# Input units in pairs: seven block products for eight on the first four row tiles, weights in operands of two tiles

## The chip, the cores and the metric

One core of a Trainium2 chip runs the whole program. The metric is the device time of one execution in microseconds (us). Before the change it is 3091.2 us, the median of three runs (3088.71 to 3091.31). The profiled execution, from which every duration below is read, spans 3091.2 us as well.

## The reference, cut to what matters

Two layers of an encoder work on 768 tokens: a sample of 512 and a prompt of 256. All arithmetic is in fp32.

```
for l in range(2):
    h = rmsnorm(x, norm_pre[l])
    parts = split(h @ w_in[l])            # 2048 -> 56 units of 128 columns, and decays
    y_a = gated_delta_net(...)            # 4 heads, both directions, chunks of 64 tokens;
                                          # triangular_solve(I + a_low, ...) per chunk
    y_b = differential_attention(...)     # 4 heads, rotary, two softmaxes each
    y_c = b * dwconv3(c * x) * silu(z)    # 4 units of 128 channels
    y_m = attention(q, mem_k, mem_v)      # 4 heads; keys and values = rmsnorm(mem) @ w_kv
    x = x + rmsnorm(concat(y_a, y_b, y_c, y_m) @ w_out[l], norm_post[l])
```

The products h @ w_in, mem @ w_kv and y @ w_out have 2048 rows each, which is 16 row tiles of 128.

## The kernel before

**Products.** Activations lie with features on the partitions and tokens along the row. A *unit* is 128 output columns: 56 input units per layer (a list `UNITS` sets their order), 8 units for keys and values of the memory, 16 output units. Each fp32 operand is cut into a leading part `hi` and a remainder `lo` of TensorE's fp32r type, and a product of two is three products: hi·hi, hi·lo, lo·hi. For each of the 16 row tiles (`k`) of a unit TensorE (PE) so issues three products, and each of them twice, because a PSUM bank takes 512 columns: once over the sample's 512 tokens and once over the prompt's 256 (L220, `GROUPS`). One row tile of an input unit is three pairs of 512 and 256 columns. A unit's sums stay in PSUM (`pp`), from where the branches read them.

**Weights.** They come in quarters of four row tiles (128x512, 256 KB): SyncE (SP) issues the load (`raw`, L159), ScalarE (ACT) casts the leading part (`hi`, L170), and VectorE (DVE) subtracts it (`lo`, L181). `run_jobs` issues these a few quarters ahead of the products.

**Order.** Everything else is a set of Python generators. `tick()` lets each of them issue its next stage, and `run_jobs` calls it once per quarter of an input unit. So the work of the branches stands on each engine's queue at a place that is counted in quarters of products; each engine takes its queue in order, and where a row's input is late, the engine stands still and all behind it with it. `until()` ticks on without products where a product's input has not been issued yet.

**The inverse on GpSimd (POOL).** A head of the delta net needs inverses of unit triangles. PE's products at L738 close the matrices, DVE and POOL copy their 32x32 diagonal blocks (L783, L784), these go through DRAM (`ud`, `ul`) into a layout of 48 partitions, and POOL runs 30 rounds of a multiply (L796) and an add (L798) there, three rounds per tick. The result goes back through DRAM (`xd`, `c`), is copied into place (L820, L821, L822 to L825), and PE carries on with small products at L833. In the same stretch POOL does the rotary embedding of the next head of differential attention (L962, L965, L967) and the remainder of its keys (`bkl`, L1037), which PE reads at L1068.

**Memory attention.** `mem` loads a head's keys and values from DRAM (`mkv`), splits them (L1127, L1128), and makes three passes of 256 tokens: scores (L1151), maximum (L1154, L1155), exponentials (L1158), scaling (L1164), transposition (L1170) with split (L1172, L1173), product with the values (L1181), gate (L1183).

**Storage.** Parts of activations (`h`) have a pool of their own (`hp`), other tiles one of 25 slots (`wk`).

Of the kernel before, what the change touches and what calls it, by code (L numbers as in the profile page):

```python
# [52 lines left out]
NRAW = 4  # L53
NF = 3
TICK = 0.6


class Job:
    """Four quarters of products of one weight unit with the activations."""

    def __init__(self, src, segs, out, done=None, ready=None, start=None,
                 dense=False):
        self.src, self.segs, self.out, self.done, self.ready = src, segs, out, done, ready
        self.start, self.dense = start, dense
        self.w = [None] * 4


class Pair:
    """The accumulators of the two groups, where they are in separate tiles."""

    def __init__(self, new):
        self.new, self.t = new, {}

    def __getitem__(self, key):
        o = key[1].start
        if o not in self.t:
            self.t[o] = self.new()
        return self.t[o][:, 0:key[1].stop - o]
# [7 lines left out]
class Trunk:  # L86
    def __init__(self, ctx, tc, io):
# [3 lines left out]
        self.hp = ctx.enter_context(tc.tile_pool(name="hp", bufs=KT))  # L91
# [6 lines left out]
        self.jobs = []  # L98
        self.room = 4

# [10 lines left out]
    def ppt(self):  # L111
        return self.pp.tile([P, 1024], F32, tag="pp", name=self.nm("pp"))
# [7 lines left out]
    def hslot(self, g):  # L120
        return self.hp.tile([P, 2, GROUPS[g][1]], F32R, tag=f"h{g}", name=self.nm(f"h{g}"))

# [8 lines left out]
    def tick(self):  # L131
        """Issues the next stage of every background task that is due."""
# [21 lines left out]

    def wload(self, i):
        if i < len(self.quarters):
            job, q = self.quarters[i]
            rf = self.wp.tile([P, 4, P], F32, tag="raw", name=self.nm("raw"), bufs=NRAW)
            self.nc.sync.dma_start(rf, job.src[:, 4 * q:4 * q + 4, :])  # L159
            job.w[q] = rf  # L160

    def whi(self, i):
        """The leading part, in F32R, of a quarter of a weight unit."""
        if i >= len(self.quarters):
            return
        nc = self.nc
        job, q = self.quarters[i]
        rf = job.w[q]
        hi = self.wp.tile([P, 4, P], F32R, tag="hi", name=self.nm("hi"))
        nc.scalar.copy(hi, rf)  # L170
        job.w[q] = (rf, hi)

    def wlo(self, i):
        """What the leading part leaves of a quarter of a weight unit."""
        if i >= len(self.quarters):
            return
        nc = self.nc
        job, q = self.quarters[i]
        rf, hi = job.w[q]
        lo = self.wp.tile([P, 4, P], F32R, tag="lo", name=self.nm("lo"), bufs=3)  # L180
        nc.vector.tensor_tensor(lo, rf, hi.bitcast(F32), ALU.subtract)  # L181
        job.w[q] = (hi, lo)

    def run_jobs(self):
        nc = self.nc
        self.quarters = [(job, q) for q in range(4) for job in self.jobs[:2]]
        self.quarters += [(job, q) for job in self.jobs[2:] for q in range(4)]
        self.wload(0)
        self.tick()
        self.whi(0)  # L190
        self.wlo(0)
        nhi, nlo, nld = 1, 1, 4
        work = 1.0
        for i, (job, q) in enumerate(self.quarters):
            if q == 0 and job.start is not None:
                job.start()
# [1351 lines left out]
```

## Time and profile before

| | |
|---|---|
| median of three runs | 3091.2 us |
| span of the profiled execution | 3091.2 us |
| PE busy | 3004.3 us, 97% |
| DVE, ACT, POOL busy | 1591.0, 919.5, 879.3 us |
| chain that ended last, by engine | PE 81%, POOL 9%, DVE 4% |
| DMA | 269.83 MB, mean 87 GB/s |

A busy PE is not PE at its peak, because products are pipelined and their ends are modelled; the spacing of their starts tells what they cost. The chain of waits follows the work back from the last instruction: at each step to what released it, or else to the instruction before it on the same engine.

### The profile page before, as it was taken

What the parts mean: (1) busy time and instruction counts of PE and PEld (TensorE: products, weight loads), DVE (VectorE), ACT (ScalarE), POOL (GpSimd) and SP (SyncE); (2) the same over time, 40 slices, a digit from 0 to 9 for tenths busy, and PEclk for the clock granted to TensorE, in tenths of its full rate; (3) what the DMA queues carried; (4) which work ended last, traced back from release to release, by engine and by line L of the source; (5) the groups of instructions that cost most, each with busy time, mean ns of one, the idle gap of its engine ahead of it and who ended that gap; (6) DMA issues with size and microseconds to landing.
All of it is one profiled execution on the core that took longest, in us unless ns stands there. A gap on an engine that the chain in (4) does not pass through costs nothing.

```text
span 3091.2 us, 47316 instructions
## 1 busy us (share of the span) xinstructions
PE 3004.3 (97%) x18606; PEld 2604.7 (84%) x18606; DVE 1591.0 (51%) x2964; ACT 919.5 (30%) x1802; POOL 879.3 (28%) x1071
## 2 busy tenths in 40 slices
PE   8899999999999999999989999999999999999997
PEld 6778888888888888898867788888888888888886
DVE  6745455446345645632597554654563456455226
ACT  6422232222222232421234222322222222324112
POOL 4316214301601250310253260252117014303014
PEclk9899999999999999999999999999999999999998
DMA  6322222212212221532373222221222122224226
GB/s 236 115 69 64 62 60 81 54 56 76 75 53 72 75 57 49 169 99 65 119 246 108 65 60 62 65 79 50 74 75 64 54 69 76 57 74 152 62 62 232
DMA packets 170767, 269.83 MB, mean 87 GB/s; under 512 B 41584, under 2 KB 54128, under 8 KB 170544
## 3 DMA queue, kind: packets, MB, share of 16 engines
q1 hardware_dynamic: 169232, 265.48, 28.4%
q8 instruction: 146, 2.39, 0.3%
q10 hardware_dynamic: 1232, 1.07, 0.1%
q14 instruction: 77, 0.63, 0.1%
q0 software_dynamic: 80, 0.26, 0.0%
HBM read 233.97 MB, written 32.77 MB: 86 GB/s over the span
## 4 chain that ended last, share of the span: by engine, by line
PE 81%; POOL 9%; DVE 4%; issue 3%; DMA 1%; ACT 1%; SPq 0%; DVEq 0%; POOLq 0%; ACTq 0%
PE pp L220 69%; POOL ul L798 3%; POOL tl L796 3%; PE s L1091 1%; PE s L220 1%; DVE lo L181 1%; PE s L908 1%; PE s L528 1%; POOL bkl L1037 1%; PE s L934 1%; PE s L738 1%; PE s L921 1%; POOL sw L965 1%; PE s L1068 1%; PE s L1082 1%
## 5 line engine op out<-in xcount | busy, mean ns | idle before, releaser
L220 PE MATMUL pp<-h,hi 128*128 128x512 f32 (+1 forms) x9600 | 2185.7, 345 | 7.8 <-ACT h L364 6.3
L220 PEld LDWEIGHTS pp<-h,hi 128*128 128x128 f32 x9600 | 1513.2, 190 | 229.7 <-issue 8.8
L220 PE MATMUL pp<-h,lo 128*128 128x512 f32 (+1 forms) x4800 | 1316.0, 344 | 40.8 <-DVE lo L181 40.6
L220 PEld LDWEIGHTS pp<-h,lo 128*128 128x128 f32 x4800 | 766.2, 190 | 161.1 <-DVE lo L181 50.1
L181 DVE TENSOR_TENSOR lo<-raw,hi 128x512 fp32r<-128x512 f32 x700 | 567.5, 815 | 641.5 <-PE pp L220 430.0
L170 ACT CAST hi<-raw 128x512 fp32r<-128x512 f32 x700 | 429.7, 619 | 678.4 <-PE pp L220 562.3
L1354 POOL TENSOR_TENSOR acc<-acc,osq 128x768 f32<-128x768 f32 (+2 forms) x36 | 54.5, 1515 | 411.4 <-ACT osq L1347 403.7
L796 POOL TENSOR_TENSOR tl<-ul 48x30 f32<-48x30 f32 (+14 forms) x240 | 144.3, 601 | 90.2 <-DMA ul<-ud 59.6
L609 POOL TENSOR_TENSOR ao<-ao,hny 128x768 f32<-128x768 f32 x8 | 13.3, 1662 | 488.2 <-DVE so L605 430.9
L798 POOL TENSOR_TENSOR ul<-ul,tl 48x30 f32<-48x30 f32 (+14 forms) x240 | 146.1, 609 | 18.8
L1072 ACT ACTIVATE E<-s,bmx 128x512 f32<-128x512 f32 (+1 forms) x96 | 58.6, 614 | 201.6 <-DVE bmx L1071 190.9
L647 DVE SCALAR_TENSOR_TENSOR cva<-cv,gconv_s,cva 128x770 f32<-128x770 f32 x96 | 106.4, 1108 | 5.0
L1071 DVE TENSOR_REDUCE bmx<-s 128x1 f32<-128x512 f32 (+1 forms) x96 | 53.7, 596 | 80.5 <-PE s L1068 79.7
L679 POOL TENSOR_TENSOR gm<-masks_s,gr 128x768 fp32r<-128x768 f32 x32 | 53.9, 1712 | 118.3 <-DVE gr L565 118.3
L1339 DVE TENSOR_SCALAR ys<-pp,npost_s 128x768 f32<-128x768 f32 (+2 forms) x41 | 34.5, 841 | 98.1 <-PE pp L220 98.1
L923 ACT ACTIVATE x<-s,nD 128x128 f32<-128x128 f32 x96 | 33.6, 367 | 137.9 <-PE s L921 114.1
L725 POOL TENSOR_TENSOR U<-A,nD 128x768 f32<-128x768 f32 x16 | 27.4, 1734 | 152.1 <-DVE nD L721 152.1
L693 POOL TENSOR_SCALAR_AFFINE_SELECT A<-A 128x768 f32<-128x768 f32 x16 | 17.8, 1115 | 185.4 <-ACT A L691 185.4
L1347 ACT ACTIVATE osq<-pp 128x768 f32<-128x768 f32 (+2 forms) x38 | 25.8, 678 | 143.8 <-DVE ys L1339 143.6
L609 POOL TENSOR_TENSOR bo<-bo,hny 128x768 f32<-128x768 f32 x8 | 13.7, 1718 | 182.0 <-DVE hny L297 121.1
L1158 ACT ACTIVATE mE<-s,mmx 128x256 f32<-128x256 f32 x48 | 22.4, 471 | 131.3 <-DVE mmx L1155 129.3
L586 ACT ACTIVATE gate<-pp 128x768 f32<-128x768 f32 x32 | 26.0, 812 | 101.2 <-PE pp L220 101.2
(305 smaller groups left out, 2716.9 us busy)
## 6 DMA issues: line engine op xcount, KB each, us to landing
raw<-wu SPq DMA_DIRECT2D x472, 256.0 KB, 2.9
raw<-wo SPq DMA_DIRECT2D x164, 256.0 KB, 2.9
raw<-wkv SPq DMA_DIRECT2D x64, 256.0 KB, 4.1
y<-gate SPq DMA_DIRECT2D x24, 384.0 KB, 2.5
mem<-memT SPq DMA_DIRECT2D x32, 256.0 KB, 4.7
x<-xT SPq DMA_DIRECT2D x16, 384.0 KB, 5.3
yl<-y SPq DMA_DIRECT2D x24, 256.0 KB, 4.5
xl<-xT SPq DMA_DIRECT2D x16, 384.0 KB, 4.7
```

Source lines behind the costliest of these rows:

```text
L170: nc.scalar.copy(hi, rf)
L181: nc.vector.tensor_tensor(lo, rf, hi.bitcast(F32), ALU.subtract)
L220: nc.tensor.matmul(job.ps[:, o:o + n], w[:, j, :], job.H[g][k][:, x, :], start=(k == 0 and w is hi and x == 0), stop=(k == KT - 1 and w is ...
L647: nc.vector.scalar_tensor_tensor(a, cb[:, i:i + 770], w[:, i:i + 1], a, ALU.mult, ALU.add)
L679: nc.gpsimd.tensor_tensor(gms[d][x].rearrange("p (n c) -> p n c", n=NCH), masks[d].unsqueeze(1).to_broadcast([P, NCH, P]), dec["gs"][:, x, ...
L796: nc.gpsimd.tensor_tensor(t, ul[:, j + 1:, j:j + 1].to_broadcast([48, m, j]), ul[:, j:j + 1, 0:j].to_broadcast([48, m, j]), ALU.mult)
L798: nc.gpsimd.tensor_tensor(ul[:, j + 1:, 0:j], ul[:, j + 1:, 0:j], t, ALU.add)
L923: nc.scalar.activation(xt[:, ci, :], pb[:, ci * P:(ci + 1) * P], AF.Copy, scale=nD[:, d, n:n + 1])
L1071: nc.vector.tensor_reduce(mx[:, j:j + 1], pts[j][:, :ln], AX.X, ALU.max, negate=True)
L1072: nc.scalar.activation(E[j], pts[j][:, :ln], AF.Exp, bias=mx[:, j:j + 1], accum_out=sm[:, j:j + 1])
L1339: nc.vector.tensor_scalar(st["ys"][m][:, a:b], ps[:, a:b], self.npost[:, l, m:m + 1], None, ALU.mult)
L1354: nc.gpsimd.tensor_tensor(acc[:, o:o + n], acc[:, o:o + n], sq[:, o:o + n], ALU.add)
```

## The change

- **Halves.** The tokens are cut into two halves of 384 in place of 512 and 256. A plain row tile of an input unit is now three pairs of 384 and 384 columns.
- **Operands of two tiles.** Weights are loaded, cast and subtracted in pieces of two row tiles (128x256, 128 KB): loads L167, casts L189, subtractions L195. The list of work is now one of steps (`run_steps`), one operand each, and a tick comes when 0.6 of four row tiles' work has passed.
- **Seven products.** From the fifth unit on, input units are taken in pairs (26 per layer). The two units and the two halves of the tokens make a 2x2 block product with blocks of two row tiles for the first four row tiles. `pair_job` forms it in seven block products. It needs four sums of weight blocks (`wsum`, L182, on POOL), four combinations of activation blocks (`combine`, once per layer), and combinations of the results: copies on ACT (L308, L312), additions on DVE (L316, L321, L328, L331, L332) and two subtractions per pair on POOL (L317, L322). The other twelve row tiles are plain.
- **Copies out of PSUM.** Units no longer stay in PSUM for the branches: the combined unit lies in a slot (`u`), and the first four units are copied by ACT.
- **Storage.** One pool of 61 slots holds `h` and everything else. To make room, the delta net stores its matrices, keys, queries and values to DRAM and fetches them again (40 stores, 40 loads), transposes its keys twice, and memory attention waits (`turn`) while the last head of differential attention or the scans of a delta head are under way, and loads its keys and values only then.

The three places in the order of work that matter most follow. The first is POOL's queue at the end of the second delta head's inverse; before (`tl`, `ul` are the loop, `bkl` the remainder of keys, `U` and `w` the result):

```order
L796 TENSOR_TENSOR tl_4773<-ul_4771 48x30
L798 TENSOR_TENSOR ul_4771<-ul_4771,tl_4773 48x30
L801 AFFINE_SELECT ul_4771<-ul_4771 48x1024
L803 MEMSET ul_4771 48x32
L1037 TENSOR_TENSOR bkl_5206<-bk_4994,bks_5204 64x768
L1037 TENSOR_TENSOR bkl_5206<-bk_4994,bks_5205 64x768
L817 MEMSET w_912_5361 32x6x32
L818 MEMSET w_912_5361 32x6x32
L821 COPY U_4357<-c_900_5312 32x6x32 x4
```

and after, where L963 and L965 are the loop, L988 the copies, L1134 a rotary row that stood earlier:

```order
L963 TENSOR_TENSOR tl_5745<-ul_5743 48x30
L965 TENSOR_TENSOR ul_5743<-ul_5743,tl_5745 48x30
L1134 TENSOR_TENSOR u_6020<-u_6020,sw_6120 128x768
L968 AFFINE_SELECT ul_5743<-ul_5743 48x1024
L970 MEMSET ul_5743 48x32
L322 TENSOR_TENSOR uw_6044<-uw_6044 128x384
L182 TENSOR_TENSOR sum_6305<-raw_6235,raw_6237 128x256
L182 TENSOR_TENSOR sum_6307<-raw_6239,raw_6235 128x256
L182 TENSOR_TENSOR sum_6309<-sum_6305,raw_6239 128x256
L182 TENSOR_TENSOR sum_6311<-raw_6241,sum_6309 128x256
L1220 TENSOR_TENSOR bkl_6284<-u_6020,bks_6282 64x768
L1220 TENSOR_TENSOR bkl_6284<-u_6020,bks_6283 64x768
```

Five new rows, a combination of results and four weight sums, stand between the loop and the rows that PE reads; four more sums and two more combinations stand inside the loop.

The second is PE's queue where the first output unit of layer 0 meets the last passes of memory attention. In before the last product with the values (L1181) of the fourth head stands among the products of an input unit:

```order
L220 MATMUL pp_11664<-h_225_1035,lo_11660 128x256
L1181 MATMUL s_11785<-mPT_11703,mkvh_11496 128x256
L1181 MATMUL s_11785<-mPT_11704,mkvh_11496 128x256
L1181 MATMUL s_11785<-mPT_11703,mkv_11401 128x256
L1181 MATMUL s_11785<-mPT_11703,mkvh_11496 128x256
L1181 MATMUL s_11785<-mPT_11704,mkvh_11496 128x256
L1181 MATMUL s_11785<-mPT_11703,mkv_11401 128x256
L220 MATMUL pp_11664<-h_287_1256,hi_11658 128x512
```

and after, where L1335 are scores, L1354 transpositions and L1365 products with the values (one row of six is shown of some):

```order
L236 MATMUL pp_14417<-h_14408,lo_14438 128x384
L1354 MATMUL s_14513<-masks_s,mE_14461 128x128 x4
L1365 MATMUL s_14522<-mPT_14518,mkvh_14124 128x256
...
L1335 MATMUL s_14536<-mkvh_14532,mq_12984 128x256
...
L1354 MATMUL s_14554<-masks_s,mE_14547 128x128 x4
L1365 MATMUL s_14563<-mPT_14559,mkvh_14532 128x256
...
L236 MATMUL pp_14417<-h_14571,hi_14436 128x384 x2
```

The whole third pass, with its load of keys and values, now stands between the products of one output unit, with no other product of PE beside it.

The third is PE's queue in a pair. In before a row tile alternates the two groups of tokens:

```order
L220 MATMUL pp_11664<-h_287_1256,hi_11658 128x512
L220 MATMUL pp_11664<-h_226_1039,hi_11658 128x256
L220 MATMUL pp_11664<-h_287_1256,hi_11658 128x512
L220 MATMUL pp_11664<-h_226_1039,hi_11658 128x256
L220 MATMUL pp_11664<-h_287_1256,lo_11709 128x512
L220 MATMUL pp_11664<-h_226_1039,lo_11709 128x256
```

and after, the end of a plain row tile of the first unit, the seventh block product of the pair, and the start of a plain row tile of the second unit:

```order
L236 MATMUL pp_7536<-h_1507,lo_7657 128x384
L236 MATMUL pp_7536<-h_1348,lo_7657 128x384
L236 MATMUL pp_7509<-h_1598,hi_7655 128x384 x2
L236 MATMUL pp_7509<-h_1598,lo_7675 128x384
L236 MATMUL pp_7509<-h_1711,hi_7655 128x384 x2
L236 MATMUL pp_7509<-h_1711,lo_7675 128x384
L236 MATMUL pp_7509<-h_1403,hi_7673 128x384
L236 MATMUL pp_7509<-h_1098,hi_7673 128x384
```

A block product goes over one half of 384 columns alone (an `x2` counts two like rows), a plain row tile over both.

The core of the diff:

```diff
-NSLOT = 25
...
+TH = T // 2
+
+KS = 2
+NSLOT = 61
+NF = 2
 TICK = 0.6
...
+WBUFS = dict(raw=8, sum=4, lo=6)
+NHI = 6
+AHEAD = 5
...
+    def wsum(self, i):
+        st = self.steps[i]
+        for op in st.sums:
+            op.t = self.wtile(op, "sum")
+            self.nc.gpsimd.tensor_tensor(op.t, op.add[0].t, op.add[1].t, ALU.add)
+        self.held["raw"] -= len(st.sums) // 2
...
+        for i, st in enumerate(self.steps):
+            if st.start is not None:
+                st.start()
+            if work >= (0.3 if st.dense else TICK) or st.first:
                 self.tick()
                 work = 0.0
...
+            work += st.cost
+            upto("load", i + 1, self.wload)
...
+            upto("sum", min(i + AHEAD, 2 * i + 2), self.wsum)
+            upto("hi", min(i + AHEAD, 2 * i + 2), self.whi)
+            upto("lo", min(i + AHEAD - 1, 2 * i + 1), self.wlo)
+            upto("load", min(i + 2 * AHEAD, 2 * i + 5), self.wload)
+            if st.ready is not None:
+                self.until(st.ready)
+            op = st.op
+            terms = [(acc(), x, opens, closes) for acc, x, opens, closes in st.terms]
+            for j in range(op.n):
+                for w, part in ((op.hi, 0), (op.hi, 1), (op.lo, 0)):
+                    for acc, x, opens, closes in terms:
+                        nc.tensor.matmul(acc, w[:, j, :], x(j)[part],
...
+    def pair_job(self, srcs, H, B, done, start=(None, None), ready=None):
...
+        s1 = Operand(KS, add=(a21, a22))
+        s3 = Operand(KS, add=(a11, a21))
+        s2 = Operand(KS, add=(s1, a11))
+        s4 = Operand(KS, add=(a12, s2))
...
+        def after_p1():
+            nc.scalar.copy(u1()[:, 0:TH], ts[1][:, 0, 0:TH])
...
+        def after_p6():
+            u, w = u1()[:, TH:T], ts["w"]
+            nc.vector.tensor_tensor(w[:, TH:T], ts[1][:, 0, 0:TH], u1()[:, 0:TH], ALU.add)
+            nc.gpsimd.tensor_tensor(u, w[:, TH:T], w[:, 0:TH], ALU.subtract)
+
+        def after_p7():
+            w = ts["w"]
+            nc.vector.tensor_tensor(w[:, TH:T], ts[1][:, 0, 0:TH], w[:, TH:T], ALU.add)
+            nc.gpsimd.tensor_tensor(w[:, 0:TH], w[:, 0:TH], w[:, TH:T], ALU.subtract)
...
+        def product(op, get, x, opens, closes, after=None, **kw):
+            return Step(op, [(get, x, opens, closes)], op.n * 0.5 / 4, after=after, **kw)
...
+        steps = [product(a11, acc(1, 0), b11, True, True, after_p1, loads=[a21, a22, a11, a12], sums=[s1, s3, s2, s4],
+                         start=start[0], ready=ready, first=True),
+                 product(s1, acc(1, 1), bt("1"), True, True, after_p5, loads=[]),
+                 product(a12, acc(0, 0), b21, True, False, loads=[]),
+                 product(s2, acc(1, 0), bt("2"), True, True, after_p6, loads=[]),
+                 product(s4, acc(0, 1), b22, True, False, loads=[])]
+        steps += rest[0][:-1]
+        steps.append(product(s3, acc(1, 0), bt("3"), True, True, after_p7, loads=[]))
+        steps += rest[0][-1:]
+        steps.append(product(again, acc(1, 0), bt("4"), True, False, start=start[1], first=True))
+        steps += rest[1]
...
+    def combine(self, x1, x2, B):
...
+        nc.vector.tensor_tensor(t1, b12, b11, ALU.subtract)
+        nc.gpsimd.tensor_tensor(t3, b22, b12, ALU.subtract)
+        nc.vector.tensor_tensor(t2, t1, b22, ALU.subtract)
+        nc.vector.tensor_tensor(t4, b21, t2, ALU.add)
...
+    def turn(self):
+
+        while self.busy:
+            yield 0
...
-        while "q" not in st or "kv" not in st:
+        while "q" not in st:
             yield 0
-        q, kv = st["q"], self.mem_kv_split(st["kv"])
+        yield from self.turn()
+        kv = self.mem_kv(l, h, 0)
+        yield (0, 1)
+        q, kv = st["q"], self.mem_kv_split(kv)
         yield 0
...
+        for i in range(4, NU, 2):
+            sd = [part(*UNITS[j]) for j in (i, i + 1)]
+            start = [x[0] for x in sd]
...
+            self.pair_job([io["wu"][l, i], io["wu"][l, i + 1]], H, B, [x[1] for x in sd], start,
+                          ready=lambda: len(B["4"]) == KS)
```

## Rows read from the trace of the kernel before

**Rows 1.** The page: busy time of the engines; the chain that ended last, by engine.
```profile
PE 3004.3 (97%) x18606; PEld 2604.7 (84%) x18606; DVE 1591.0 (51%) x2964; ACT 919.5 (30%) x1802; POOL 879.3 (28%) x1071
...
PE 81%; POOL 9%; DVE 4%; issue 3%; DMA 1%; ACT 1%; SPq 0%; DVEq 0%; POOLq 0%; ACTq 0%
```

**Rows 2.** What TensorE waited for: us in total, times, longest.
```profile
PE pp L220 <- DVE lo L181: 40.6, 21, 4.9
PE s L1068 <- POOL bkl L1037: 10.9, 10, 1.5
```

**Rows 3.** Timeline of TensorE, two stretches: start, length, instructions.
```profile
14.46 0.62 PE L220 MATMUL pp<-h,hi 128*128 128x512 f32 x2
...
15.15 0.62 PE L220 MATMUL pp<-h,hi 128*128 128x512 f32 x2
...
1000.06 0.86 PE L220 MATMUL pp<-h,hi 128*128 128x512 f32 x4
...
1001.11 0.86 PE L220 MATMUL pp<-h,hi 128*128 128x512 f32 x4
```

**Rows 4.** Timeline of TensorE around the second head's inverse.
```profile
488.68 0.39 PE L738 MATMUL s<-ak 128*128 128x128 f32 x2
488.91 0.39 PE L738 MATMUL s<-aq,ak 128*128 128x128 f32 x2
...
580.77 0.22 PE L833 MATMUL s<-c,U 32*32 32x32 f32 x2
```

**Rows 5.** Timeline of GpSimd, same head; idle time before a row and its releaser in brackets.
```profile
490.25 2.24 POOL L784 COPY cd<-U 32x192 f32<-32x192 f32 x4 [15.84 <-DVE U L742]
506.03 0.25 POOL L796 TENSOR_TENSOR tl<-ul 48x30 f32<-48x30 f32 x1 [13.55 <-DMA ul<-ud]
...
517.80 1.98 POOL L962 TENSOR_TENSOR bq<-bq,rope 128x512 f32<-128x512 f32 x2 [6.15 <-DVE sw L960]
...
565.42 3.71 POOL L1037 TENSOR_TENSOR bkl<-bk,bks 64x768 fp32r<-64x768 f32 x2
...
573.83 0.45 POOL L825 COPY w<-ct 32x192 f32<-32x192 f32 x1
```

**Rows 6.** Groups by line and shape on GpSimd: count, busy us, mean ns, idle before.
```profile
L494 POOL TENSOR_TENSOR h<-ys,h 128x256 fp32r<-128x256 f32 x16 | 16.9, 1077 | 28.3 <-ACT h L493 28.3
...
L1450 POOL TENSOR_TENSOR h<-ys,h 128x256 f32<-128x256 f32 x10 | 7.8, 818 | 4.3 <-DVE ys L1448 4.3
...
L962 POOL TENSOR_TENSOR bk<-bk,rope 128x512 f32<-128x512 f32 x8 | 10.3, 1291 | 30.1 <-DVE sw L960 30.1
```

**Rows 7.** DMA issues of one kind: count, KB each, median us to landing.
```profile
mkv<-kvd SPq DMA_DIRECT2D x16, 256.0 KB, 3.3
```

**Rows 8.** Groups by line and shape of the memory attention.
```profile
L1128 DVE TENSOR_TENSOR mkv<-mkv,mkvh 128x512 fp32r<-128x512 f32 x16 | 11.0, 688 | 31.1 <-ACT mkvh L1127 31.1
...
L1154 DVE TENSOR_REDUCE mmx<-s 128x2 f32<-128x512 f32 x24 | 16.4, 684 | 31.9 <-PE s L1151 31.9
...
L1158 ACT ACTIVATE mE<-s,mmx 128x256 f32<-128x256 f32 x48 | 22.4, 471 | 131.3 <-DVE mmx L1155 129.3 <-PE s L690 2.0
...
L1164 DVE TENSOR_SCALAR mE<-mE,mrs 128x256 f32<-128x256 f32 x48 | 22.8, 516 | 0.9
...
L1173 DVE TENSOR_TENSOR mPT<-s,mPT 128x512 fp32r<-128x512 f32 x24 | 16.5, 689 | 11.2 <-ACT mPT L1172 11.0
```

**Rows 9.** Busy time per stretch, after a wait of TensorE and far from one.
```profile
569.20:573.00 3.80, 3.80 (x12) 3.18 (x13) 2.88 (x8) 1.07 (x3) 2.19 (x7) 0.58 0.92 186
1000.00:1004.00 4.00, 4.00 (x25) 3.49 (x25) 3.61 (x5) 1.69 (x5) 1.77 (x4) 1.00 0.42 131
```

**Rows 10.** VectorE: the remainders of the weights by line; a 256-column subtraction.
```profile
L181 DVE TENSOR_TENSOR lo<-raw,hi x700: 675/691/2556, 5.5 to 3069.1; 128x512 fp32r<-128x512 f32 x175
...
L181 DVE TENSOR_TENSOR lo<-raw,hi 128x512 fp32r<-128x512 f32 x700 | 567.5, 815 | 641.5 <-PE pp L220 430.0 <-issue 167.8 <-ACT hi L170 33.8
...
L742 DVE TENSOR_TENSOR U<-s,U 128x256 f32<-128x256 f32 x48 | 18.0, 417 | 27.0 <-PE s L738 27.0
```

More of the change, by code (lines that the diff above doesn't have):

```diff
@@ L97, in __init__ @@
         self.tasks = []
-        self.jobs = []
+        self.steps = []
         self.room = 4
+        self.busy = 0
     def nm(self, s):
@@ L184, in run_jobs, with preload @@
[L184 to L188, printed above, removed]
+        for op in self.steps[i].loads:
+            op.t = self.wtile(op, "raw")
+            self.nc.sync.dma_start(op.t, op.src)
+    def preload(self, n):
+        while self.done["load"] < n * 4 // KS - 1:
+            self.wload(self.done["load"])
+            self.done["load"] += 1
@@ new lines, in wlo, with run_steps, upto @@
+    def wlo(self, i):
+        op = self.steps[i].op
+        op.lo = self.wtile(op, "lo", F32R)
+        self.nc.vector.tensor_tensor(op.lo, op.t, op.hi.bitcast(F32), ALU.subtract)
+        self.held["sum" if op.src is None else "raw"] -= 1
+    def run_steps(self):
+        nc = self.nc
+        n = len(self.steps)
+        done = self.done = dict(load=0, sum=0, hi=0, lo=0)
+        self.held = dict.fromkeys(WBUFS, 0)
+        def upto(what, i, f):
+            while done[what] < min(i, n if what == "load" else done["load"]):
+                if what == "load" and not self.wfits(done[what]):
+                    return
+                f(done[what])
+                done[what] += 1
+        upto("load", 1, self.wload)
@@ L189, in run_jobs @@
         self.tick()
-        self.whi(0)
-        self.wlo(0)
-        nhi, nlo, nld = 1, 1, 4
+        upto("hi", 1, self.whi)
+        upto("lo", 1, self.wlo)
         work = 1.0
-        for i, (job, q) in enumerate(self.quarters):
-            if q == 0 and job.start is not None:
-                job.start()
-            if work >= (0.3 if job.dense else TICK) or q == 0:
+        for i, st in enumerate(self.steps):
+            if st.start is not None:
+                st.start()
+            if work >= (0.3 if st.dense else TICK) or st.first:
@@ new lines, in run_steps, with chunks, parts, job @@
+            self.held["lo"] -= 1
+            if st.after is not None:
+                st.after()
+        self.until(lambda: not self.tasks)
+    def chunks(self, a):
+        n = -(-(KT - a) // KS)
+        cuts = [a + (KT - a) * i // n for i in range(n + 1)]
+        return list(zip(cuts, cuts[1:]))
+    def parts(self, H, g, k):
+        return H[g][k][:, 0, :], H[g][k][:, 1, :]
+    def job(self, src, segs, out, H, done=None, ready=None, start=None, dense=False, width=TH, parts=None):
+        parts = parts or self.parts
+        ps = []
+        def acc(g):
+            def get():
+                if not ps:
+                    ps.append(out())
+                return ps[0][:, g, 0:width]
+            return get
+        steps = []
+        for a, b in self.chunks(0):
+            op = Operand(b - a, src[:, a:b, :])
+            terms = [(acc(g), lambda j, g=g, a=a: parts(H, g, a + j), a == 0, b == KT) for g in segs]
+            steps.append(Step(op, terms, len(segs) * width / T * (b - a) / 4, ready=ready and (lambda b=b: ready(b)),
+                              start=start if a == 0 else None, dense=dense, first=a == 0,
+                              after=(lambda: done(ps[0])) if b == KT and done else None))
+        self.steps += steps
```

364 lines of the change are left out of this document (203 added, 161 removed).

## Prediction

> **What bounds the kernel now.** I read the page first: PE is busy for 97% of the span and makes 81% of the chain that ended last, with POOL second at 9% [rows 1]. So a product saved on PE is time saved, as long as nothing else comes late. The list of PE's waits says how near that is: 40.6 us in 21 waits for `lo` from DVE, 10.9 us for POOL's `bkl` [rows 2]. The reader is to see that these two engines, at 51% and 28%, gate PE already at a few places. Then the timelines. PE's: a row tile of an input unit takes 1.05 us from start to start, three pairs of 512 and 256 columns at 0.350 us; in a memory unit three products of 512 columns take 0.69 us, 0.23 each [rows 3]. And POOL's around an inverse, against PE's places there: PE closes the matrices at 488.9, POOL's last copy ends at 574.3, PE reads it at 580.8 [rows 4, 5]. The slack of this chain is 6.5 us of 92. It decides my forecast.
>
> **Products.** Per pair of units seven block products take the place of eight; a block product is two row tiles by three products on one half, so six products of 384 columns go per pair, 312 in all (52 pairs). 384 columns are half of the pair of 0.350 us, 0.175 us each [rows 3]. 312 x 0.175 = 54.6 us saved. Whether two halves of 384 cost just what 512 and 256 do no row shows. The bounds: by the memory unit's 0.23 for 512, 0.350 leaves 0.12 for 256, and a line through both gives 0.175 again, so 0; if cost went with columns alone from the 0.23 row, 0.172 each, so 13,512 products save 40 us at most, and a small row at 0.12 for 256 speaks for the line. I take -10, bounds -40 and +10.
>
> The 48 transpositions done twice: two 128x128 products start 0.23 us apart [rows 4], 0.11 each, 5.3 us.
>
> **The inverse on POOL.** This is the largest term. PE's distance from the last L738 to L833 holds, by the order, 240 pairs (480 products) and 26 small ones in the heads 2 and 3 of each layer: 240 x 0.350 + 3.4 = 87.4 us; the trace has 91.9 [rows 4], of which some 4 are the wait for `bkl` (10.9 us over six heads [rows 2]) and the clock behind it (below). After the change the same distance holds 408 products of 384 columns and some 20 small ones: 408 x 0.175 + 2.6 = 74 us. It shrinks by 13 us because ticks come nine to a pair of units in place of eight, while the chain is counted in ticks.
>
> The chain on POOL in before: 17.1 us from 488.9 to the loop's first row (copies, DRAM and back), 59.4 us to the row behind the loop (565.4), 8.8 us for `bkl`, the way through DRAM and the copies [rows 4, 5]: 85.4 us. New on it: one group of four sums and three results' rows inside the loop and behind it, another group of four sums before `bkl`. A sum of 128x256 costs between 0.82 and 1.08 us by the nearest rows [rows 6]; I take 0.95, four 3.8. A result row of 384 columns lies between 0.82 and 1.29 [rows 6]; I take 1.0. So 59.4 + 3.8 + 3.0 = 66.2; behind the loop 3.8 + 3.7 (`bkl`) + 4.4 (the fills and copies) = 11.9 in place of 8.8, because what used to hide under DRAM no longer fits there. 17.1 + 66.2 + 11.9 = 95.2 us. Against that, POOL's 6.15 us of waiting inside the loop for DVE's `sw` [rows 5] goes when POOL itself is late: 89.0. PE waits 89 - 74 = 15 us per head; bounds 21 (that wait stays) and 0 to 8 (new rows at their shortest, and the 17.1 shrinks with the ticks, which order alone can't tell). Heads 1 and 4 have 77.7 and 76.1 us of PE's work there by the same count, but PE reads their `bkl` sooner; I take 15 for these too. 8 x 15 = 120, less the 10.9 that PE waits for `bkl` already: +109. What else stands behind POOL then: sums for the next pair of units, and ACT's casts of them, so the wait may show at L236 just as well as at L1000 or L1253. It is one lateness, paid once.
>
> **Ends of the layers.** In before the third pass of memory attention lies between products of input units and costs PE nothing. After, it waits for differential attention's last head, and the first output unit waits for it. Its own length: load 3.3 [rows 7], split 0.6 + 0.7, scores 0.7, maximum 0.7 + 0.4, two exponentials 0.9 + 0.4, two scalings 1.0, transpositions 0.5, split 0.6 + 0.7, products 0.7, gate 0.4, its split 0.6: 12.2 us. The 0.69, 0.68, 0.47 and 0.52 are of [rows 8]; what has no row there is my estimate from its like. Nothing of PE stands beside it. 2 x 12 = +24, bounds 0 (earlier passes finish sooner than the order suggests) and 36 (half of the second pass shows too).
>
> **Clock.** After the wait at 569.2 the granted clock is 0.58 of full speed over the next 3.8 us, most of it at 1.2 GHz, where 12 products fit; far from a wait, 25 fit in 4.0 us at 1.00 [rows 9]. 12 x 0.16 = 1.9, so 1.9 us are lost per wait. Ten long waits (eight heads, two ends) take the place of those for `bkl` in six heads, and some heads will have two. I count six more, +11.
>
> **Edits at nothing.** ACT takes casts and copies on top of 919.5 us [rows 1], and stays under half. Loads double in number, but carry the same bytes. DVE: 1540 subtractions of 256 columns at 0.42 in place of 700 at 0.69 [rows 10], 647 for 483 us, or 830 for 568 if each meets the excess that a mean of 815 over a median of 691 shows; 260 additions of results at 0.5 to 0.7, 130 to 180. DVE comes to some 1,900 to 2,000 us of 3,100; the products hide it except where PE waits for `lo` already; see rivals. The last group's end has 384 columns for 256, ten rows on POOL at 0.82 [rows 6] become some 1.2: +4.
>
> **Sum**, against the profiled 3091.2, which is also the median: -54.6 - 10 + 5.3 + 109 + 24 + 11 + 4 = +89, so 3180 us.
>
> **A rule weighed.** L181 takes 675 ns at its shortest, 691 at the median, 2556 at its longest [rows 10], so something holds it. The Trainium skill (SBUF — State Buffer, the section on SBUF's two separate sides) says that a DVE operation with two SBUF inputs and a GpSimd operation that reads SBUF share a pair of ports under an exclusive lock for a whole instruction, and the second fully blocks. The trace agrees with a block rather than a slower rate, since the median stays near the minimum. By that rule the blocks go with the number of instructions on both sides, 1540 and 1399 for 700 and 1076, not with columns, which is the rival on DVE below.
>
> **Rivals.**
> 1. *POOL's lateness does not reach PE.* The chain must fall from 89 to 74 us per head, for which the 17.1 us before the loop and the sums would have to shrink together. For it: POOL is busy for 28% only, 15.8 and 13.6 us of the chain are idle [rows 5]. Against: the idle stretches are DRAM and ticks, which the order keeps. Then 3091.2 - 54.6 - 10 - 10.9 + 5.3 + 24 + 4 = 3049: faster.
> 2. *Half of it*: 7 us per head, from rows at their shortest. 120 becomes 56, clock 6: 3180 - 64 - 5 = 3111.
> 3. *DVE comes late too*, by the blocks. `lo` is there one or two steps ahead of its product, and a step is now 1 us (a block product) where a quarter was 4.2. If PE's 40.6 us for `lo` [rows 2] double and POOL's rows are 10% longer in the eight stretches (8 x 6 us): 3180 + 41 + 48 = 3269. For it: `lo` is already the longest wait. Against: shorter rows let go of the ports sooner.
>
> **Chances.** Forecast 0.47, rival 1 0.16, rival 2 0.19, rival 3 0.18. The forecast's own range is 3145 to 3230. The range that holds 8 in 10 leaves out rival 1 and the far side of rival 3: 3080 to 3265. This kernel tells a difference of 0.2%, 6 us, from none. Faster: rival 1 and a little of rival 2, 0.17; same 0.04; slower 0.79.
>
> **What would show it.** Right: PE idles about 15 us near each of the eight inverses, with POOL (sums, L1220, L988) as releaser directly or through ACT; POOL has no idle time in its loops; 12 us of idle at each layer's first output unit; row tiles still at 1.05 us. Wrong: POOL's loop ends as early against PE as before, or PE's idle time lies with L195 spread over all pairs, or row tiles take another time.

## The result and the profile after

The changed kernel takes 3268.7 us (median of four runs, 3268.1 to 3269.7), before 3090.0 on the same chip: a ratio of 1.0577, 95% interval 1.0562 to 1.0592. That is 179 us slower, where 90 were forecast (3180, range 3080 to 3265). The side was right, the size was not: twice as much, and outside the range.

The page of the changed kernel, busy times and the chain that ended last, answers to [rows 1]:

```profile
PE 3033.3 (93%) x18342; PEld 2887.5 (88%) x18342; DVE 2048.0 (63%) x4084; ACT 1087.5 (33%) x2754; POOL 1110.4 (34%) x1394
...
PE 69%; POOL 13%; DVE 8%; issue 4%; DMA 2%; ACT 2%; SPq 0%; DVEq 0%; POOLq 0%; ACTq 0%
```

PE's share of the chain falls from 81% to 69%; POOL's rises from 9% to 13%, DVE's from 4% to 8%. The list of PE's waits answers to [rows 2]:

```profile
PE pp L236 <- DVE lo L195: 72.4, 57, 4.3
PE s L1253 <- POOL bkl L1220: 43.5, 12, 10.4
PE pp L236 <- ACT u L308: 41.6, 52, 2.1
PE s L1354 <- DVE mE L1348: 16.9, 8, 3.1
PE pp L236 <- DVE uw L321: 11.9, 6, 2.9
...
PE s L1000 <- DMA c<-xd: 7.2, 4, 2.4
```

(Each row: us in total, number of waits, the longest.) The wait for `bkl` was forecast. The third row was not: 52 waits, one in each pair. Nor were the first and the fourth at this size. The rows that go back to POOL (`bkl`, L321, `c`) come to 62.6 us, some 8 per inverse where 15 were forecast.

The inverse of the second head on POOL's timeline, idle time in brackets, answers to [rows 5]:

```profile
513.69 1.68 POOL L951 COPY cd<-U 32x192 f32<-32x192 f32 x4 [9.22 <-DVE U L894]
527.89 2.62 POOL L317 TENSOR_TENSOR u<-uw 128x384 f32<-128x384 f32 x1 [12.51 <-DVE lo L195]
534.62 0.24 POOL L963 TENSOR_TENSOR tl<-ul 48x30 f32<-48x30 f32 x1 [4.12 <-DMA ul<-ud]
...
576.87 0.99 POOL L317 TENSOR_TENSOR u<-uw 128x384 f32<-128x384 f32 x1
...
590.26 1.01 POOL L322 TENSOR_TENSOR uw<-uw 128x384 f32<-128x384 f32 x1
591.24 1.93 POOL L182 TENSOR_TENSOR sum<-raw,raw 128x256 f32<-128x256 f32 x2
...
595.02 3.86 POOL L1220 TENSOR_TENSOR bkl<-u,bks 64x768 fp32r<-64x768 f32 x2
...
602.38 0.44 POOL L992 COPY w<-ct 32x192 f32<-32x192 f32 x1
```

and PE's on the same stretch, to [rows 4]:

```profile
509.58 0.39 PE L890 MATMUL s<-aq,ak 128*128 128x128 f32 x2
...
578.59 0.58 PE L236 MATMUL pp<-h,hi 128*128 128x384 f32 x2 [2.89 <-DVE uw L321]
...
589.27 0.85 PE L236 MATMUL pp<-h,hi 128*128 128x384 f32 x4
...
593.48 0.86 PE L236 MATMUL pp<-h,hi 128*128 128x384 f32 x4
...
595.73 0.25 PE L1000 MATMUL s<-c,U 32*32 32x32 f32 x4 [1.04 <-DMA c<-xd]
...
598.93 0.38 PE L1253 MATMUL s<-bkl,bqs 64*128 64x256 f32 x1 [1.46 <-POOL bkl L1220]
```

From PE's last closing product (509.6) to POOL's last copy (602.8) are 93 us, where 89 to 95 were worked out. But PE's first product on the result (L1000, 595.73) starts 7 us before that copy ends: it waits for the data to come back from DRAM, not for POOL's copies, which the forecast counted into the chain. PE needs 86 us to this product where 74 were worked out without waits, so 12 us of waits and slow clock, where 15 were forecast. The waits among these 12 are 7.5 us, and 3.9 of them go back to POOL: 1.04 for the result and 2.89 for L321. In that second one POOL's L317 stands behind rounds of the loop (576.87), DVE's L321 may not overwrite what L317 still reads, and PE may not reuse the PSUM that L321 has yet to read (578.59):

```profile
577.89 0.56 DVE L321 TENSOR_TENSOR uw<-pp,uw 128x384 f32<-128x384 f32 x1 [2.54 <-POOL u L317]
```

The wait in each pair, ACT and PE at a pair's start:

```profile
518.75 0.48 ACT L308 COPY u<-pp 128x384 f32<-128x384 f32 x1 [1.90 <-PE pp L236]
```
```profile
518.38 0.33 PE L236 MATMUL pp<-h,lo 128*128 128x384 f32 x1
519.28 0.62 PE L236 MATMUL pp<-h,hi 128*128 128x384 f32 x2 [0.57 <-ACT u L308]
```

The second block product of a pair (519.28) writes the other bank of the same two-bank PSUM tile. It starts only when ACT has copied the first product's result out (518.75 + 0.48): 0.90 us from start to start in place of 0.175.

Clock, a wait of PE and busy time per stretch after it, answers to [rows 9] (the granted clock is the third number from the end of a row):

```profile
302.18 0.58 PE L1253 MATMUL s<-bkl,bqs 64*128 64x256 f32 x1 [9.44 <-POOL bkl L1220]
```
```profile
302.20:306.00 3.80, 2.50 (x6) 1.99 (x7) 1.29 (x3) 1.43 (x5) 3.49 (x5) 0.50 0.05 16
306.00:313.00 7.00, 6.43 (x19) 4.96 (x18) 2.26 (x5) 1.57 (x4) 5.90 (x15) 0.50 0.07 21
315.00:319.00 4.00, 4.00 (x25) 3.97 (x24) 3.52 (x9) 2.28 (x8) 1.04 (x1) 1.00 0.37 110
```

After the wait of 9.4 us that ends at 302.2 PE stays at 1.2 GHz (0.50) to 313, with two short waits between; in before the stretch after a wait of 1.5 us was 3.8 us at 0.58.

The end of layer 0 on PE's timeline:

```profile
1333.70 0.34 PE L236 MATMUL pp<-h,lo 128*128 128x384 f32 x1
...
1337.06 1.09 PE L1354 MATMUL s<-masks_s,mE 128*128 128x128 f32 x4 [3.02 <-DVE mE L1348]
...
1346.23 1.12 PE L1354 MATMUL s<-masks_s,mE 128*128 128x128 f32 x4 [2.69 <-DVE mE L1348]
...
1349.98 0.52 PE L236 MATMUL pp<-h,hi 128*128 128x384 f32 x1
```

For 16.3 us, between two products of an output unit, PE has nothing but memory attention; 7.6 us of them are waits. 12 us were forecast.

What was right: four plain row tiles (589.27 to 593.48) take 4.21 us, 1.05 each as before, so 384 columns cost 0.175 us. Equal halves gained nothing: over all neighbouring products at a granted clock of 1.00 the median from start to start is 0.175 us, and 0.232 for 512 and 0.117 for 256 columns in before, which makes 0.350 a pair against 0.349. Groups by shape, to [rows 2], [rows 6] and [rows 10]:

```profile
L236 PE MATMUL pp<-mh,lo 128*128 128x512 f32 x256 | 108.1, 422 | 25.3 <-DVE lo L195 25.3
...
L195 DVE TENSOR_TENSOR lo<-raw,hi 128x256 fp32r<-128x256 f32 x1332 | 810.7, 635 | 317.8 <-ACT hi L189 309.9 <-DMA raw<-wkv 4.3 <-DMA mem<-memT 1.7
...
L182 POOL TENSOR_TENSOR sum<-raw,raw 128x256 f32<-128x256 f32 x104 | 84.1, 822 | 2.4 <-DMA raw<-wu 1.3
...
L317 POOL TENSOR_TENSOR u<-uw 128x384 f32<-128x384 f32 x52 | 56.1, 1079 | 585.0 <-DVE uw L316 499.2 <-ACT E L1257 60.5 <-ACT hi L189 12.5
```

A sum costs 0.82 us (0.95 was taken), a result row 1.08 (1.0 taken).

### The profile page after: what moved, and what is told of

It is laid out like the page before. It is cut to its first block, busy times and chain, and to the rows that moved or that the text cites. A ratio compares the mean times of both kernels' runs of the same rounds, so it can differ in the third digit from the quotient of the medians.

```text
span 3266.4 us, 52353 instructions
## 1 busy us (share of the span) xinstructions
PE 3033.3 (93%) x18342; PEld 2887.5 (88%) x18342; DVE 2048.0 (63%) x4084; ACT 1087.5 (33%) x2754; POOL 1110.4 (34%) x1394
## 4 chain that ended last, share of the span: by engine, by line
PE 69%; POOL 13%; DVE 8%; issue 4%; DMA 2%; ACT 2%; SPq 0%; DVEq 0%; POOLq 0%; ACTq 0%
PE pp L236 58%; POOL ul L965 4%; POOL tl L963 4%; DVE lo L195 2%; PE s L1276 1%; PE s L1075 1%; POOL ys L1602 1%; POOL sw L1132 1%; POOL u L1129 1%; POOL u L1134 1%; PE s L1088 1%; POOL bkl L1220 1%; PE s L682 1%; PE s L1101 1%; POOL sum L182 1%
## 5 line engine op out<-in xcount | busy, mean ns | idle before, releaser
L236 PE MATMUL pp<-h,hi 128*128 128x384 f32 x9008 | 2097.6, 344 | 55.3 <-ACT u L308 41.6
L236 PEld LDWEIGHTS pp<-h,hi 128*128 128x128 f32 x9008 | 1615.7, 191 | 86.8 <-ACT u L308 59.3
L236 PE MATMUL pp<-h,lo 128*128 128x384 f32 x4504 | 1268.5, 342 | 47.3 <-DVE lo L195 47.1
L195 DVE TENSOR_TENSOR lo<-raw,hi 128x256 fp32r<-128x256 f32 x1332 | 810.7, 635 | 317.8 <-ACT hi L189 309.9
L236 PEld LDWEIGHTS pp<-h,lo 128*128 128x128 f32 x4504 | 837.4, 191 | 63.3 <-DVE lo L195 62.6
L189 ACT CAST hi<-raw 128x256 fp32r<-128x256 f32 x1332 | 496.4, 406 | 522.5 <-PE pp L236 443.7
L317 POOL TENSOR_TENSOR u<-uw 128x384 f32<-128x384 f32 x52 | 56.1, 1079 | 585.0 <-DVE uw L316 499.2
L322 POOL TENSOR_TENSOR uw<-uw 128x384 f32<-128x384 f32 x52 | 56.7, 1090 | 422.0 <-DVE uw L321 419.2
L195 DVE TENSOR_TENSOR lo<-sum,hi 128x256 fp32r<-128x256 f32 x208 | 118.6, 584 | 108.8 <-ACT hi L189 108.6
L963 POOL TENSOR_TENSOR tl<-ul 48x30 f32<-48x30 f32 (+14 forms) x240 | 130.1, 542 | 39.3 <-DMA ul<-ud 24.6
L965 POOL TENSOR_TENSOR ul<-ul,tl 48x30 f32<-48x30 f32 (+14 forms) x240 | 134.8, 562 | 18.8
L189 ACT CAST hi<-sum 128x256 fp32r<-128x256 f32 x208 | 83.5, 407 | 152.6 <-POOL sum L182 95.6
L236 PE MATMUL pp<-mh,lo 128*128 128x512 f32 x256 | 108.1, 422 | 25.3 <-DVE lo L195 25.3
L236 PE MATMUL pp<-mh,hi 128*128 128x512 f32 x256 | 108.0, 422 | 9.6 <-ACT mh L496 9.6
L236 PE MATMUL pp<-ml,hi 128*128 128x512 f32 x256 | 106.1, 414 | 0.5 <-DVE ml L497 0.5
L331 DVE TENSOR_TENSOR u<-pp,uw 128x384 f32<-128x384 f32 x52 | 28.9, 556 | 96.8 <-PE pp L236 96.8
```

Of the source, the lines that this page charges most:

```text
L189: self.nc.scalar.copy(op.hi, op.t)
L195: self.nc.vector.tensor_tensor(op.lo, op.t, op.hi.bitcast(F32), ALU.subtract)
L236: nc.tensor.matmul(acc, w[:, j, :], x(j)[part], start=opens and j == 0 and w is op.hi and part == 0, stop=closes and j == op.n - 1 and w i ...
L317: nc.gpsimd.tensor_tensor(u, w[:, TH:T], w[:, 0:TH], ALU.subtract)
L322: nc.gpsimd.tensor_tensor(w[:, 0:TH], w[:, 0:TH], w[:, TH:T], ALU.subtract)
L963: nc.gpsimd.tensor_tensor(t, ul[:, j + 1:, j:j + 1].to_broadcast([48, m, j]), ul[:, j:j + 1, 0:j].to_broadcast([48, m, j]), ALU.mult)
```

## The experiments

Each is compared with the kernel before on its own chip (3089.4 to 3092.4 us). A difference between two of them is that of their medians; runs of one kernel differ by up to 14 us.

**1. Order of two products (e1_order).** The product with a12, which writes another PSUM tile, goes between the two.

```diff
-                 product(s1, acc(1, 1), bt("1"), True, True, after_p5, loads=[]),
                  product(a12, acc(0, 0), b21, True, False, loads=[]),
+                 product(s1, acc(1, 1), bt("1"), True, True, after_p5, loads=[]),
```

> The changed kernel with one edit: in a pair the product with a12 stands second and the one with s1 third. Theory P (PE waits 0.8 us in each of the 52 pairs because the s1 product may not write its bank before ACT has copied the first product's result out of the same PSUM tile, 41.6 us in the list of waits): that entry goes to under 5 us and the time falls by 40 to 55 us, to about 3220. Theory Q (those waits only take up lateness that the chain on POOL would show anyway): the entry goes too, but other waits grow and the time falls by less than 15 us.

3232.5 us, 36 under the changed kernel:

```profile
PE pp L236 <- ACT uw L312: 6.8, 12, 0.6
PE pp L236 <- ACT u L308: 5.7, 8, 0.8
PE pp L236 <- DVE u L332: 3.8, 24, 0.2
```

PE's wait for L308 goes from 41.6 to 5.7 us; L312 and L332, the next to read those PSUM tiles out, are new in the list. The loss is there, as theory P has it, but somewhat under its 40 to 55 us. The edit also gives the first weight sum one step more; that share was not taken apart.

**2. No block products (e2_plain).**

```diff
-        for i in range(4, NU, 2):
-            sd = [part(*UNITS[j]) for j in (i, i + 1)]
...
+        for i in range(4, NU):
+            s, d = part(*UNITS[i])
...
+            self.job(io["wu"][l, i], (0, 1), self.ppt, H, start=s, done=evac(d))
```

> The changed kernel without the block products: the 52 units per layer after the first four run one by one with eight plain operands of two tiles, without sums and combinations; all else (halves of 384, slots, spills, turn) stays. Theory A (the block products bring the loss): PE's own work grows by 312 x 0.175 = 55 us, the ticks are eight per two units again, and the time is 3090 to 3130. Rival B (operands of two tiles, spills and turns bring it): 3200 or more.

3157.3 us: neither. The block products, with their nine ticks per pair in place of eight, cost 111 us net although they save 55 us of PE's work; the rest of the change costs 65.

**3. Two subtractions from POOL to DVE (e3_dve).**

```diff
-            nc.gpsimd.tensor_tensor(u, w[:, TH:T], w[:, 0:TH], ALU.subtract)
+            nc.vector.tensor_tensor(u, w[:, TH:T], w[:, 0:TH], ALU.subtract)
```

(and the one in `after_p7` likewise)

> The changed kernel with the two subtractions of results per pair (L317, L322) on DVE in place of POOL. Theory C (DVE's L321 may not overwrite the result that POOL's L317 still reads, L317 stands behind the loop of the inverse, and so PE waits for PSUM that L321 should free): PE's wait for L321 (11.9 us) goes, POOL has 113 us less, the wait for bkl falls from 43 to under 30 us; time 3220 to 3245. Rival D (DVE is the engine that comes late): DVE gets 57 us more, its waits grow, and the time stays or rises.

3261.3, only 7 less: far from theory C's range and nearer to rival D, though DVE's own waits hardly grow (`lo` 72.4 to 74.0). The wait for L321 falls to 1.1, `bkl` to 36.5; the wait for the result (L1000) grows from 7.2 to 11.6, and ACT's casts (L189) are new with 9.2. The chain is there still.

**4. Seven ticks per pair (e4_ticks).**

```diff
-            if work >= (0.3 if st.dense else TICK) or st.first:
+            if work >= (0.3 if st.dense else 0.8 if getattr(st, "slow", False) else TICK) or st.first:
```

> The changed kernel with a tick in a pair only when 0.8 of four row tiles' work has passed: seven ticks per pair in place of nine. Theory T (the chain on POOL is counted in ticks, and nine ticks per pair leave PE too little work beside it): PE's distance beside an inverse grows by a quarter, 74 to some 92 us, the waits for bkl (43.5 us) and for the inverse (7 us) all but go, and with them their clock; if nothing else came late, some -70 us. Against it work is pushed to the ends of the layers: +10 to +40 us there. Sum 3200 to 3250. Rival D (DVE's and PSUM's waits spread over the pairs make the loss): within 15 us of the changed kernel.

3305.1, 36 slower. The waits for `bkl` and the inverse left the list, as theory T says, but the wait for L308 rose from 41.6 to 95.5 (6.7 us the longest) and the work pushed to the layers' ends is waited for there. A miss: pace alone only moves the loss. Before one of the long waits a cast of a weight sum on ACT (L189, 895.86) has stood still for 14.5 us until POOL made the sum, and the copy L308 (899.55) stands behind it in ACT's queue. So POOL's lateness still reaches PE, through ACT.

**5. `bkl` on DVE (e5_bkl).**

```diff
-            nc.gpsimd.tensor_tensor(kl[a], t[a], s[a].bitcast(F32), ALU.subtract)
+            nc.vector.tensor_tensor(kl[a], t[a], s[a].bitcast(F32), ALU.subtract)
```

> The changed kernel with the remainder of the keys (bkl, L1220) on DVE in place of POOL. Theory C (chain on POOL: bkl stands behind the loop and the sums): PE's wait for bkl (43.5 us in 12 waits) all but goes, the clock behind it recovers, DVE gets 16 instructions more; 3210 to 3230. Rival D (lateness of many parts): the wait moves to other rows of the same heads and the time falls by less than 15 us.

3249.4, 19 less, between the two theories. The wait for `bkl` goes, but that for L308 grows to 62.1 with two of 10.6 us: half of it is waited for elsewhere. ACT's timeline before the first of them (PE carries on at 305.27) shows the same way as in experiment 4:

```profile
299.75 0.41 ACT L189 CAST hi<-sum 128x256 fp32r<-128x256 f32 x1 [12.48 <-POOL sum L182]
...
304.73 0.49 ACT L308 COPY u<-pp 128x384 f32<-128x384 f32 x1
```

**6. Half of the loop (e6_half).**

```diff
         for j in range(1, 31):
-            m = 31 - j
...
+            if j % 2 == 0:
+                m = 31 - j
...
```

> The changed kernel with every second round of POOL's loop left out (30 instructions of 60 per head; the inverse is incomplete), ticks unchanged. Theory C: 8 heads have some 18 us less on POOL; the waits near the inverses that POOL causes (bkl, the copies, L321 behind L317) go, about 60 to 70 us with their clock: 3195 to 3215. The waits for lo behind DVE's rows and for L308 stay. Rival D (POOL is not what is late): less than 20 us.

3169.1, 100 less, and the list of PE's waits has nothing of `bkl` or of the inverse left and 0.4 us of L321. It begins:

```profile
PE pp L236 <- DVE lo L195: 70.1, 56, 4.3
PE pp L236 <- ACT u L308: 42.2, 52, 2.1
PE s L1355 <- DVE mE L1349: 16.8, 8, 3.0
```

So POOL's lateness is worth some 100 us with its clock, more than theory C's 60 to 70: 63 us less idle time of PE (span less busy, 233.1 to 169.8) and 36 us by quicker products (busy 3033.3 to 2997.8, at a mean granted clock of 0.981 in place of 0.966). That the shorter loop helps by letting DVE go on is ruled out: the subtractions L195 did not get shorter (mean 635 to 649 ns).

**7. Half of the loop without block products (h4_plainhalf)**, the edits of 2 and 6 together.

> The version without block products (e2_plain, 3157 us) with every second round of POOL's loop left out (the inverse is incomplete). Theory C: the loop is late only because the pairs' sums and subtractions and their shorter distance stand against it; without pairs, half a loop gives under 12 us: 3145 to 3157. Rival: the loop is late by the slots, spills or fetches of the rest of the change; then 40 us or more, as in the pair version (99).

3146.9, 10 less than e2_plain, as theory C has it: beyond these 10 us the loop is late only with the pairs.

**8. Operands of four tiles, without block products (e9_plain4).**

```diff
-KS = 2
+KS = 4
...
-WBUFS = dict(raw=8, sum=4, lo=6)
-NHI = 6
-AHEAD = 5
+WBUFS = dict(raw=4, sum=1, lo=3)
+NHI = 4
+AHEAD = 3
```

> The version without block products (e2_plain, 3157 us) with operands of four row tiles (128x512, 256 KB) as in the kernel before. Theory E (pieces of two tiles cost DVE, ACT and queues, and leave PE waiting): back to within 20 us of the kernel before, 3095 to 3115. Rival F (the ends of the layers, with turn and spills, make the 65 us): 3145 to 3160, the waits at the ends unchanged.

3230.0: 73 slower than e2_plain, and against both. Waits for `lo` rise from 49 to 78 us, for `bkl` from 7 to 28. So going back to four tiles, with these buffers and this look-ahead, is a loss here. Whether the size itself does it is not shown: a shorter look-ahead, fewer buffers and longer rows on DVE change at once.

**9. No turn, without block products (e7p_noturn).**

```diff
-        yield from self.turn()
```

> The version without block products (e2_plain, 3157 us) where memory attention does not wait its turn. Rival F: the waits at the two ends (some 36 us in e2_plain with their clock) go, 3115 to 3130. Theory E: less than 10 us.

3126.5, 31 less than e2_plain, as rival F has it. In e2_plain PE waits at the layer's end for the passes of memory attention (the first three rows); without turns none of these is left there. What is left (the last two rows) is the wait for differential attention's `ao`, which e2_plain has too (5.81 us), and a short one for ACT:

```profile
1273.49 1.11 PE L1351 MATMUL s<-masks_s,mE 128*128 128x128 f32 x4 [1.27 <-DVE mE L1345]
...
1281.49 1.09 PE L1351 MATMUL s<-masks_s,mE 128*128 128x128 f32 x4 [2.78 <-DVE mE L1345]
...
1290.68 1.12 PE L1351 MATMUL s<-masks_s,mE 128*128 128x128 f32 x4 [2.71 <-DVE mE L1345]
```
```profile
1277.20 1.54 PE L769 MATMUL s<-masks_s,ao 128*128 128x128 f32 x6 [5.91 <-POOL ao L760]
1279.71 1.28 PE L236 MATMUL pp<-h,hi 128*128 128x384 f32 x2 [0.96 <-ACT h L459]
```

The version with block products was not run without turns.

**10. The edits of 1 and 6 together, and the order of issue (g1_orderhalf, g5_halfall, g3_swapearly, g4_all).** g1 has the edits of 1 and 6. In the profile after, one wait in each of six heads reads like this on DVE and PE:

```profile
523.06 1.51 DVE L950 STREAM_TRANSPOSE cd<-U 32x192 f32<-32x192 f32 x4
524.60 0.76 DVE L195 TENSOR_TENSOR lo<-sum,hi 128x256 fp32r<-128x256 f32 x2
525.08 0.69 PE L236 MATMUL pp<-h,lo 128*128 128x384 f32 x1 [2.42 <-DVE lo L195]
```

From 517.70 on DVE had a tick's rows to do, and the subtraction stood behind them. g5 (g1 with this edit) and g3 (e1_order with it) issue it ahead of them; g4 is g3 with the edit of 5:

```diff
-            if work >= (0.3 if st.dense else TICK) or st.first:
-                self.tick()
...
             upto("load", min(i + 2 * AHEAD, 2 * i + 5), self.wload)
+            if work >= (0.3 if st.dense else TICK) or st.first:
+                self.tick()
...
```

> The changed kernel with the order of e1_order and the half loop of e6_half (every second round of POOL's loop left out, the inverse is incomplete). If PSUM's wait and the chain on POOL are two separate losses, they add: 3169 - 36 = 3133 within 6. If one takes up the other, 3145 to 3169. What is then left over the kernel before, less the products saved, some 40 + 50 us, must have another cause.

3147.7: 21 less than e6_half, where 36 would be two separate losses; they share a part. (Its runs lie 14 us apart.)

> g1_orderhalf (with its incomplete inverse), and in run_steps the weight sums, casts and subtractions ahead are issued before the tick of a step in place of behind it. Theory D2 (what is left are waits for lo of 0.9 to 2.6 us near the heads, where DVE's queue has 5 to 6 us of a tick's rows ahead of a subtraction that is only four steps of 1 us ahead of its product): waits for lo fall from some 70 to under 45 us, time 20 to 40 us under g1_orderhalf. Rival G (DVE's rate, not its order): within 8 us.

3115.4: 32 less than g1_orderhalf; waits for `lo` 70.2 to 44.5. Theory D2 holds.

```profile
PE pp L236 <- DVE lo L195: 44.5, 29, 4.3
```

> e1_order with the issue before the tick, whole loop. Theory D2: 20 to 35 us under e1_order (3233), so about 3205. Rival G: within 8 us. As the sums on POOL then stand ahead of the tick's rows, the wait for bkl may grow by up to 8 us.

3211.8, 21 less than e1_order: the lower end. `lo` falls from 71.9 to 42.0, but L321 rises from 10.8 to 18.7 and `mE` from 16.8 to 24.0.

> g3_swapearly with bkl on DVE. If the gain of e5_bkl (19 us) adds to it: some 3185. If the lateness of POOL only shows elsewhere (the copies L988, L321 behind L317): 3195 to 3205.

3198.1, 14 less, inside the second range: POOL's lateness shows elsewhere. The 40.9 us for `bkl` are gone, those for L321 and L332 rise from 25.4 to 48.7.

**11. Block products away from the inverses only (h1_mixed), against the plain version with the same order of issue (h2_plainearly), and that without turns (h3_plainall).**

```diff
         for i in range(4, NU, 2):
+            if i in (6, 8, 10, 18, 20, 22, 32, 34, 36, 46, 48, 50):
+                for j in (i, i + 1):
+                    s, d = part(*UNITS[j])
+                    self.job(io["wu"][l, j], (0, 1), self.ppt, H, start=s, done=evac(d))
+                continue
```

> e2_plain (3157 us) with the issue before the tick. In the pair version this gave 21 us; here a step is 2.1 us long, so less is late: 5 to 20 us, 3137 to 3152.

3143.3: 14 less than e2_plain, as expected.

> Block products only in the 14 of 26 pairs per layer that lie away from the inverses; the 12 pairs beside them run as plain units; a12 second, issue before the tick. If POOL beside an inverse is what eats the products' gain, then 28 pairs x 6 products x 0.175 us = 29 us arrive in full against the plain version with the same issue order (h2_plainearly): some 3105. If a pair loses as much elsewhere (DVE's additions, copies, clock), the same as h2 or slower.

3153.7, 10 slower than h2_plainearly, where 29 us of PE's work are saved: the second case, a pair loses as much elsewhere, and POOL beside the inverses isn't all. PE waits for memory attention's `mE` 32.1 us in place of 13.5.

> e7p_noturn (plain, no turn, 3126 us) with the issue before the tick: 3107 to 3121 if the two add. What then remains over the kernel before, 15 to 30 us, is the spills, transpositions and copies.

3109.0: 34 less than h2_plainearly, as expected: the best of all these and still 18 over the kernel before, which no version beat.

**12. What eats the rest (i1_narrow, i2_mixedhalf).** i1 is g5_halfall with L321 and L328 over 8 columns per half (L321 is shown):

```diff
-            nc.vector.tensor_tensor(w[:, TH:T], ts[1][:, 0, 0:TH], w[:, TH:T], ALU.add)
+            nc.vector.tensor_tensor(w[:, TH:TH + 8], ts[1][:, 0, 0:8], w[:, TH:TH + 8], ALU.add)
```

> g5_halfall (3115 us, incomplete inverse), and two of DVE's five additions of results per pair (L321, L328) go over 8 and 2 x 8 columns only, so that most of those results lack a term. It takes some 50 us from DVE and keeps order and waits. If DVE's load from the pairs is what is left, 10 to 25 us: 3090 to 3105. If it is not, within 6 us.

3117.3, no change, with 46 us less on DVE. DVE's load from these additions isn't the cause.

> h1_mixed (3154 us) with every second round of POOL's loop left out (the inverse is incomplete). POOL is not late beside the inverses there, if the theory holds: within 12 us, as in the plain version (10 us). 30 us or more would say that the few block products away from the inverses still load POOL at the wrong time.

3135.9, 18 less than h1_mixed: between the two. A little of POOL's lateness is left there.

## Why the forecast fell short, step by step

- **Products.** Right: 312 fewer, at 0.175 us. The 10 us for equal halves were not there.
- **The inverse on POOL.** The mechanism was right: POOL comes late, and only with the pairs (100 by the half loop, 10 with the pairs gone). The size of the wait was not. 109 us more of waits were forecast; the three rows that go back to POOL come to 62.6, 52 more than before. Part of the reason is that POOL's fills and copies (4.4 us in the sum) do not stand before PE's next product. That 109 + 11 and 100 lie so near is luck: a third of the 100 is slow clock. "One lateness, paid once" was wrong too: it is paid in several waits, through L1253, L1000 and L321, and through ACT where those are taken away.
- **Ends of the layers.** 24 forecast, 12 at each end, in a place where PE now spends 16 us on memory attention alone; 31 by taking the turns away, in the version without block products.
- **A step that failed: "Edits at nothing".** It costed the copies and additions of results and the shorter look-ahead at nothing, on the ground that ACT and DVE are half idle. Two losses lay there, and neither is load. First, the copy L308 holds up the next product in each pair, because both use one PSUM tile: 41.6 us of waits, 36 us of time alone, 21 once POOL is out of the way. The order of PE and ACT in a pair showed it, and no term of the sum spoke of PSUM. Second, DVE's subtractions stood behind a tick's rows, with a look-ahead that in block products is three steps of 1 us (not four, as expected for g5_halfall) in place of two quarters of 4.2: 21 to 32 us by order of issue alone, while 46 us less load on DVE changed nothing.
- **A step that failed: "Clock".** 11 us were forecast, six more waits at 1.9 us. By the mean granted clock (0.988 of 3091.2 us, 0.966 of 3266.4) some 37 us were lost to it before and some 111 after, an estimate: 74 more. PE's busy time says the same: 29 us more, for some 50 us less work. This is the largest single shortfall of the sum. The price was read after a wait of 1.5 us; after that of 9.4 the clock stayed at 1.2 GHz for 11 us, and there are many more waits than six.
- **How the parts add up.** PE's idle time (span less busy) grew by 146 us, from 87 to 233, where 137 were forecast (109 + 24 + 4). This sum came out by luck: 42 us for L308 and 32 more for `lo` stand where half of POOL's 109 was expected. With 74 for the clock and some 50 of work saved it gives 170 of the 179 us.
- **Rival 3** gave 3269, the time that came out, by doubled waits for `lo` and POOL's rows 10% longer. The first half came true in part, by order more than by blocks: 40.6 us of waits became 72.4, 25.3 of them in the memory units. The second didn't: the loop's two lines came down from means of 601 and 609 ns to 542 and 562. So the time is no proof of that rival.
- **The ports.** The median of L195 is 421 ns and its longest 3545, for 691 and 2556 before: still blocks and not a slower rate, as the Trainium skill has it (SBUF — State Buffer, the section on two separate sides: one of the two engines fully blocks). By the number of instructions, 1540 x 0.124 = 191 us of excess were to be had; the means of 635 and 584 over medians near 420 give some 320. PE's time didn't follow it: in g5_halfall the mean was 676, in a kernel 153 us faster.

Taken away one after the other, half the loop, the order of a12 and the issue before the tick give 100 + 21 + 32 = 153 of the 179 us. Left are 25, and the some 50 us of products that should then show as a gain. The turns account for 31 of these 75 if they cost in the pair version what they cost in the plain one, which was not run. Some 40 are open. h1_mixed points at memory attention, whose stages, counted in ticks, PE reaches sooner in a pair; that was not tested.

## What to carry to other kernels

A transform that saves products also shortens the time in which everything else has been hidden; count that time again beside each long chain on another engine. Price each new wait with the slow clock behind it, which here cost about half as much again as the idle time itself. Then look at each new result of PE: who reads it out, and which product next needs its PSUM tile. A half idle engine is no cover where its queue has the urgent row behind the others; put that row first before you count its load.

## What was not expected of the hardware

After a wait of 9.4 us PE ran 11 us at 1.2 GHz, with two short waits (1.30 and 0.57 us) between, against under 4 us after one of 1.5 us; over the whole span the granted clock fell from 0.988 to 0.966 by the view by core. Operands twice as long, with their look-ahead and buffers changed along, made the kernel without block products 73 us slower (3230 against 3157); that this is the hardware's doing is not shown.
